# A four-layer diffusion transformer on one core: one operation less in the differential bias, shared accumulation for the last units, earlier splits of gated tiles

## The chip, the core and the metric

The program runs on one NeuronCore of a Trainium2 chip. The metric is the device time of one execution in microseconds (us). The engines are TensorE (PE; its weight loads are PEld), VectorE (DVE), ScalarE (ACT), GpSimd (POOL) and SyncE (SP, which issues the transfers). A lower time is better.

## What is computed

Four layers (`DEPTH = 4`) act on 1024 latent tokens and 256 context tokens, each 1024 wide, batch one. Layer i uses the mixer i mod 3: A (grouped-query attention, layers 0 and 3), B (neighbourhood attention with a learned bias, layer 1), C (differential attention, layer 2).

```
def diff_attention(q, k, v, lam):
    scale = HEAD_DIM ** -0.5
...
        logits = jnp.einsum("bqhmd,bkhmd->bhmqk", qb, k).astype(jnp.float32) * scale
        p = jax.nn.softmax(logits, axis=-1)
        a = (p[:, :, 0] - lam * p[:, :, 1]).astype(v.dtype)
        return jnp.einsum("bhqk,bkhd->bqhd", a, v)
```

Every layer does: modulated norm, one input projection to the mixer's q, k, v and a SiLU gate, the mixer, the gate times the mixer's output, an output projection, a gated residual. Layers 0 to 2 also carry the context tokens; layer 3 only produces the latent ones. In layer C each head has two softmax maps over context and latent keys, and the second, times a learned `lam`, is added to the first (the kernel's `lam` carries the sign). Each softmax subtracts the row's maximum, so the exponential's bias is `-SC` times the largest score over context and latent keys.

## The kernel before

**Numbers and layout.** Matmuls that need more than one pass of accuracy take each operand as a rounded high part and a low remainder: `round_pool` (L130, on POOL) writes the high part, `sub` (L133, on DVE) subtracts it from the original and writes the low part. `whi` and `wlo` are such parts of a weight, the two `ogt` buffers are those of a gated tile. Tokens go in tiles of 128, eight latent and two of context.

**Layers A (0 and 3).** Attention is done in units: a pair of heads for a block of up to 512 query tokens, over 10 key blocks for latent queries, 2 for context ones. Units come in the order in which the groups `g` = 0 to 3 are written. For each key block PE writes the transposed scores `st` (L714, L715), ACT exponentiates them to `p` (L719, 128x1024), PE accumulates `o` (L739). The softmax's denominator is the sum of all `p` of the unit: POOL adds most of them into one accumulator (L753), DVE adds the last ones into a second (the same line, `side` = 1), and `mixed` (L757) multiplies `o` by the gate and adds the two accumulators (L761). Then `spread` multiplies the sum by ones on PE (`sum`, L767), ACT turns it into a reciprocal, `error` and `step` refine it (DVE, ACT), and `over` (L788, L789, POOL) multiplies it into `og`, the gated output. These last five steps of the last unit are the tail: `unit_events` returns it in `self.tail`, and `out_proj` emits it.

Only PE's instructions are pinned in the order in which they are written in layers A; what stands where on the other engines is the scheduler's choice. In layers B and C (`tile_events`) all four compute engines are pinned in the order of the events' times.

**Output projection.** `out_proj` (L875) loops over the work list: the first 512 output columns of every tile, then the second 512. For each entry it needs the gated tile in two parts (`split`: four blocks of 256 columns, so 4 instructions L130 on POOL and 4 L133 on DVE) and does 24 matmuls `y` (L911): 8 slices of the inner dimension by three part products. The split of the next tile is written ahead of the products of the present one. The evacuation is DVE (`yg`, L950), POOL (`xo`, L951), and a transfer.

**Layer C.** A tile is 128 queries of one head. For each, `near` writes the context scores `sc` of both maps, takes their maxima `mx` (L1456, a 128x2 result) and multiplies `mx` by `-SC` (L1457). `scores(m)` writes the latent scores of map m, takes their maximum `ml` (L1466, a 128x1024 reduction) and combines it with `mx` by multiplying with `-SC` and taking the minimum (L1467), one per map. ACT exponentiates with `mx` as bias. `sums` makes the row sums and their ratio `rs` (L1404, L1405), DVE combines half of the latent probabilities (L1492), POOL the context ones and the other half (`combine`: L1412 multiplies by `rs`, L1413 adds). PE turns the result (`pT`) and multiplies by the values.

## Time and profile before

| what | value |
|---|---|
| time, median of 3 runs | 3613.51 us (3613.27 to 3614.67) |
| profiled execution, its own time | 3609.91 us |
| its span | 3608.1 us |
| mean granted clock of PE | 0.985 |
| PE busy | 3471.8 us, 96% |
| PEld, DVE, POOL, ACT busy | 72%, 57%, 53%, 37% |

The span is what the trace covers; 1.8 us of the execution's own time lie around it. The profiled execution is 3.6 us (0.1%) under the median of the runs. All instants below are microseconds from the start of that span. PE is busy for almost the whole span, so that the time of the kernel is PE's work and PE's waits; the stretches where PE waits are short and lie at particular places: the ends of the four attentions (around 838, 1686, 2715 and 3505) among them.

### The profile page before, as it was taken

To read this page: it belongs to the slowest core of one execution; us is meant where nothing else is said; L and a number is where in the kernel's file an instruction comes from. 1 tells how busy PE (TensorE), PEld (TensorE's weight loads), DVE (VectorE), ACT (ScalarE), POOL (GpSimd) and SP (SyncE) were. 2 spreads that over 40 slices of the span, in tenths; PEclk is the share of its full clock that TensorE was granted. 3 is DMA by queue.
4 is the path that set the end of the run, shared out by engine and by line. 5 is a ranking of instruction groups with operands and counts; after the bars stand their busy time and mean duration, and the time that the engine had idled before them with its cause. 6 is when DMAs were issued, how large, how long until landed. Compare 5 with 4: busy or idle time off the path is not lost.

```text
span 3608.1 us, 49956 instructions
## 1 busy us (share of the span) xinstructions
PE 3471.8 (96%) x18594; PEld 2608.3 (72%) x18594; DVE 2057.5 (57%) x3358; ACT 1320.9 (37%) x2756; POOL 1915.1 (53%) x1854
## 2 busy tenths in 40 slices
PE   7999999998999999999999999999999999999989
PEld 4887444446788888887878888888887787554447
DVE  5552555665641412888566610799994654466653
ACT  3221444451321212774222211677771322344430
POOL 5540666677531311667565510566775643377884
PEclk9999999999999999999999999999999999999999
DMA  6343443513344434552425531221312335111113
GB/s 211 78 122 101 140 138 113 192 56 97 122 105 129 111 123 113 169 153 69 146 79 140 136 114 56 84 82 44 96 42 95 120 79 142 47 40 44 45 41 88
DMA packets 229453, 370.33 MB, mean 103 GB/s; under 512 B 34088, under 2 KB 124120, under 8 KB 229212
## 3 DMA queue, kind: packets, MB, share of 16 engines
q1 hardware_dynamic: 228636, 367.01, 34.5%
q8 instruction: 147, 2.41, 0.3%
q14 instruction: 94, 0.77, 0.1%
q10 hardware_dynamic: 576, 0.15, 0.0%
HBM read 270.36 MB, written 96.57 MB: 102 GB/s over the span
## 4 chain that ended last, share of the span: by engine, by line
PE 73%; DVE 14%; POOL 7%; issue 3%; ACT 1%; DMA 1%; SPq 0%; POOLq 0%; ACTq 0%; DVEq 0%
PE proj L382 22%; PE zT L467 11%; PE y L911 9%; PE o L739 7%; PE st L714 4%; PE st L715 4%; DVE ml L1466 3%; PE sl L670 2%; PE o L1136 2%; POOL p L753 2%; DVE wlo L133 1%; PE qkT L437 1%; POOL rstd L146 1%; PE ada L195 1%; PE pT L1214 1%
## 5 line engine op out<-in xcount | busy, mean ns | idle before, releaser
L753 POOL TENSOR_TENSOR p<-p,p 128x1024 f32<-128x1024 f32 x224 | 540.1, 2411 | 303.6 <-PE o L739 258.2
L382 PE MATMUL proj<-whi,hhi 128*128 128x512 f32 x1408 | 556.3, 395 | 3.7 <-POOL whi L130 2.4
L382 PE MATMUL proj<-wlo,hhi 128*128 128x512 f32 x1408 | 550.8, 391 | 3.0 <-DVE wlo L133 3.0
L382 PE MATMUL proj<-whi,hlo 128*128 128x512 f32 x1408 | 550.4, 391 | 0.0
L719 ACT ACTIVATE p<-st 128x1024 f32<-128x1024 f32 (+1 forms) x336 | 324.1, 1003 | 286.2 <-PE st L715 274.3
L911 PE MATMUL y<-whi,ogt 128*128 128x512 f32 x1216 | 387.5, 396 | 13.2 <-POOL ogt L130 9.4
L661 DVE TENSOR_REDUCE M<-sl 128x1 f32<-128x512 f32 (+1 forms) x326 | 209.8, 685 | 293.2 <-PE sl L670 243.5
L133 DVE TENSOR_TENSOR wlo<-wraw,whi 128x1024 fp32r<-128x1024 f32 x136 | 217.3, 1612 | 221.6 <-POOL whi L130 196.3
L739 PE MATMUL o<-p,v 128*64 128x512 f32 x1344 | 321.2, 599 | 0.0
L130 POOL TENSOR_SCALAR whi<-wraw 128x1024 fp32r<-128x1024 f32 x136 | 178.7, 1319 | 252.6 <-DMA wraw<-in_c_w_in_dram 86.0
L382 PEld LDWEIGHTS proj<-whi,hhi 128*128 128x128 f32 x1408 | 265.7, 189 | 57.9 <-POOL whi L130 2.6
L382 PEld LDWEIGHTS proj<-wlo,hhi 128*128 128x128 f32 x1408 | 265.6, 189 | 57.6 <-DVE wlo L133 4.7
L382 PEld LDWEIGHTS proj<-whi,hlo 128*128 128x128 f32 x1408 | 265.3, 188 | 55.2
L911 PEld LDWEIGHTS y<-whi,ogt 128*128 128x128 f32 x1216 | 229.8, 189 | 67.8 <-POOL ogt L130 11.6
L467 PE MATMUL zT<-hhi,whi 128*128 128x512 f32 (+1 forms) x704 | 256.9, 365 | 5.6 <-DVE qklo L133 5.6
L404 ACT ACTIVATE y<-proj 128x1024 f32<-128x1024 f32 (+1 forms) x68 | 65.6, 964 | 527.0 <-PE proj L382 469.4
L467 PE MATMUL zT<-hhi,wlo 128*128 128x512 f32 (+1 forms) x704 | 254.5, 362 | 1.3 <-DVE wlo L133 1.3
L467 PE MATMUL zT<-hlo,whi 128*128 128x512 f32 (+1 forms) x704 | 254.5, 362 | 0.0
L911 PE MATMUL y<-wlo,ogt 128*128 128x512 f32 x608 | 238.6, 392 | 0.0
L146 POOL TENSOR_TENSOR rstd<-rstd,mhalf 128x16 f32<-128x16 f32 (+3 forms) x132 | 231.0, 1750 | 10.9
L714 PE MATMUL st<-q,k 128*128 128x512 f32 x512 | 217.8, 425 | 10.5 <-DVE M L658 7.2
L658 DVE TENSOR_REDUCE M<-sl 128x2 f32<-128x1024 f32 (+1 forms) x165 | 200.6, 1216 | 45.2 <-PE sl L670 40.1
(221 smaller groups left out, 7035.2 us busy)
## 6 DMA issues: line engine op xcount, KB each, us to landing
adaw<-in_ada_w_dram SPq DMA_DIRECT2D x96, 512.0 KB
xo<-xres SPq DMA_DIRECT2D x86, 256.0 KB
wraw<-in_a_w_in_dram SPq DMA_DIRECT2D x40, 512.0 KB
k<-k SPq DMA_DIRECT2D x40, 512.0 KB
q<-qkhi SPq DMA_DIRECT2D x76, 256.0 KB
q<-qklo SPq DMA_DIRECT2D x76, 256.0 KB
q<-q SPq DMA_DIRECT2D x136, 128.0 KB
wraw<-in_b_w_in_dram SPq DMA_DIRECT2D x32, 512.0 KB
```

The costliest lines, as they stand in the source:

```text
L130: self.nc.gpsimd.tensor_scalar(out=out, in0=in_, scalar1=1.0, scalar2=0.0, op0=ALU.mult, op1=ALU.add)
L133: self.nc.vector.tensor_tensor(out, a, b, op=ALU.subtract)
L146: nc.gpsimd.tensor_tensor(r, r, self.mhalf[:, :n], op=ALU.pow)
L382: nc.tensor.matmul(ps[:, i, :], self.h_op(a, 2 * tp + i, k), wop(b, k), start=(k == 0 and j == 0), stop=(k == KT - 1 and j == 2),)
L467: nc.tensor.matmul(ps, wop(a, k)[:, b * P : (b + 1) * P], self.h_cols(c, g, k), start=(k == 0 and j == 0), stop=(k == KT - 1 and j == 2),)
L658: nc.vector.tensor_reduce(out=out, in_=both.rearrange("p (h q k) -> p h q k", h=2, q=n), axis=AX.X, op=ALU.max)
L661: nc.vector.tensor_reduce(out=out[:, hh, :], in_=ps[hh].rearrange("p (q k) -> p q k", q=n), axis=AX.X, op=ALU.max)
L714: nc.tensor.matmul(ps[:, hh, :], self.k_op(K, 0, kt), q1[:, hh, :], start=True, stop=False)
L719: nc.scalar.activation(p, ps, AF.Exp, scale=HD**-0.5)
L739: nc.tensor.matmul(st["o"][hh * HD : (hh + 1) * HD, :], v(hh, kt), p[:, hh, :], start=j == 0, stop=j == N - 1, tile_position=(0, hh * HD),)
L753: eng.tensor_tensor(a, a, p, op=ALU.add)
L911: nc.tensor.matmul(ps, ot[a][:, k, :], wop[h](b, k), start=(k == 0 and j == 0), stop=(k == KT - 1 and j == 2))
```

## The change

There are five edits.

1. In layer C the multiplication of `mx` by `-SC` (L1457) is dropped. The combination in `scores` becomes one `tensor_scalar`: the larger of `ml` and the column `mx[:, m]`, times `-SC`. Before, it was a `scalar_tensor_tensor` with two tensor operands and a constant; now it has one tensor operand, a per-partition scalar that is read from memory, and a constant.
2. In layers A the number of key blocks that DVE adds is an argument, `share`: 5 for the units of the last group with `t0 > 0` (two units in each of the layers 0 and 3), 2 for all others as before. Of the 10 blocks of such a unit POOL adds 4 instead of 7 times, DVE 4 times instead of once.
3. Splitting a tile is a method, `split_tile`. In layers 0, 1 and 3 (`kind < 2`) the first two gated tiles are split by events at 0.965 to 0.99 of the attention's length.
4. In `out_proj`, layer 2's first two tiles are split inside the loop behind the first step of the weights' second half.
5. The tail of the last unit is emitted behind the second `y` tile (`i > 0`) instead of behind the first.

```diff
-            side = int(j > 0 and j >= N - 2)
+            side = int(j > 0 and j >= N - share)
...
+    def split_tile(self, t):
+
+        if t in self.halves:
+            return
+        self.halves[t] = hi, lo = [self.slot([P, KT, P], F32R, "ogt") for _ in range(2)]
+        g, o = t // 4, (t % 4) * P
+        for b in range(4):
+            a = self.og.block(b, g)[:, :, o : o + P]
+            h, l = (x[:, 2 * b : 2 * b + 2, :] for x in (hi, lo))
+            self.round_pool(h, a)
+            self.sub(l, a, h)
+
...
-        start(0)
         for i, (h, t) in enumerate(work):
             cs = slice(h * 512, h * 512 + 512)
             if i < len(steps):
                 steps[i]()
-            if i + 1 < len(work):
-                start(i + 1)
+            for x in work[i : i + 2]:
+                self.split_tile(x[1])
...
-            products(ps, h, halves[t] if h == 0 else halves.pop(t), range(KT))
-            while self.tail:
+            products(ps, h, self.halves[t], range(KT))
+            while self.tail and i > 0:
                 self.tail.pop(0)()
...
-                        2 * g + pr, t0, n, kts, self.finish_plain,
+                        2 * g + pr, t0, n, kts, 5 if g == 3 and t0 else 2, self.finish_plain,
...
-                nc.vector.tensor_scalar_mul(mx, mx, -SC)
...
-                nc.vector.scalar_tensor_tensor(
-                    out=mx[:, m : m + 1], in0=ml, scalar=-SC, in1=mx[:, m : m + 1], op0=ALU.mult, op1=ALU.min
+                nc.vector.tensor_scalar(
+                    out=mx[:, m : m + 1], in0=ml, scalar1=mx[:, m : m + 1], scalar2=-SC, op0=ALU.max, op1=ALU.mult
                 )
...
+            if kind < 2:
+                extra.append((0.965, 0.99, [lambda t=t: self.split_tile(t) for t in range(2)]))
             self.og = self.Mixed(self)
+            self.halves = {}
```

The order of the instructions moves at three places that matter below.

On POOL at the end of layer 0's attention before the change (the `p` are accumulations, `r` and `og` the end of the unit before, `whi` weights, `ogt` the splits of the first two gated tiles):

```order
L753 TENSOR_TENSOR p_6213<-p_6213,p_6220 128x1024
L753 TENSOR_TENSOR p_6213<-p_6213,p_6234 128x1024
L753 TENSOR_TENSOR p_6213<-p_6213,p_6241 128x1024
L753 TENSOR_TENSOR p_6213<-p_6213,p_6263 128x1024
L753 TENSOR_TENSOR p_6213<-p_6213,p_6272 128x1024
L788 TENSOR_TENSOR r_6252<-r_6252,e_6265 128x512
L789 TENSOR_TENSOR og_626<-og_626,r_6252 128x512
L753 TENSOR_TENSOR p_6213<-p_6213,p_6296 128x1024
L753 TENSOR_TENSOR p_6213<-p_6213,p_6303 128x1024
L130 TENSOR_SCALAR whi_6371<-wraw_6185 128x1024
L130 TENSOR_SCALAR ogt_6439<-og_617 128x256
```

The same place on POOL with the change:

```order
L753 TENSOR_TENSOR p_6212<-p_6212,p_6219 128x1024
L753 TENSOR_TENSOR p_6212<-p_6212,p_6234 128x1024
L753 TENSOR_TENSOR p_6212<-p_6212,p_6241 128x1024
L753 TENSOR_TENSOR p_6212<-p_6212,p_6263 128x1024
L788 TENSOR_TENSOR r_6252<-r_6252,e_6265 128x512
L789 TENSOR_TENSOR og_626<-og_626,r_6252 128x512
L130 TENSOR_SCALAR ogt_6349<-og_617 128x256
```

Three accumulations are gone from POOL's queue, and the split of the first gated tile stands directly behind `og`. On DVE the last unit's accumulations stand with the change like this, among the low parts of the two tiles:

```order
L753 TENSOR_TENSOR p_6272<-p_6272,p_6296 128x1024
L753 TENSOR_TENSOR p_6272<-p_6272,p_6303 128x1024
L133 TENSOR_TENSOR ogt_6350<-og_617,ogt_6349 128x256
L133 TENSOR_TENSOR ogt_6350<-og_620,ogt_6349 128x256
L133 TENSOR_TENSOR ogt_6350<-og_622,ogt_6349 128x256
L133 TENSOR_TENSOR ogt_6350<-og_625,ogt_6349 128x256
L753 TENSOR_TENSOR p_6272<-p_6272,p_6329 128x1024
L133 TENSOR_TENSOR ogt_6385<-og_617,ogt_6384 128x256
L753 TENSOR_TENSOR p_6272<-p_6272,p_6336 128x1024
L133 TENSOR_TENSOR ogt_6385<-og_620,ogt_6384 128x256
L759 TENSOR_TENSOR og_626<-o_6243,og_626 128x512
L761 TENSOR_TENSOR p_6212<-p_6212,p_6272 128x1024
```

All four accumulations are DVE's now, and the tail's sum (L761) comes behind one and a half split tiles.

On DVE at the end of layer 1's attention before the change (`ptl` copies turned probabilities out of PE's banks, `mx` is the last latent tile's maximum, the two ISA operations add the bias and take maxima, `mc` is the maximum for the context queries):

```order
L1215 COPY ptl_14572<-pT_14573 128x768
L1162 TENSOR_REDUCE mx_14592<-sc_14587 128x2
L1173 ISA p_14599,ml_14600<-st_14594,biasb_14032 128x256
...
L1197 RECIPROCAL rs_14620<-rs_14620 128x2
L1215 COPY ptl_14633<-pT_14634 128x768
L1243 TENSOR_REDUCE mc_14657<-sc_14648 128x4
```

The same place on DVE with the change (lines stand 10 earlier in the file):

```order
L1205 COPY ptl_14572<-pT_14573 128x768
L133 TENSOR_TENSOR ogt_14588<-og_9876,ogt_14587 128x256
L133 TENSOR_TENSOR ogt_14588<-og_10035,ogt_14587 128x256
L133 TENSOR_TENSOR ogt_14588<-og_10217,ogt_14587 128x256
L133 TENSOR_TENSOR ogt_14588<-og_10270,ogt_14587 128x256
L1152 TENSOR_REDUCE mx_14602<-sc_14597 128x2
...
L1187 RECIPROCAL rs_14630<-rs_14630 128x2
L1205 COPY ptl_14643<-pT_14644 128x768
L133 TENSOR_TENSOR ogt_14653<-og_9876,ogt_14652 128x256
L133 TENSOR_TENSOR ogt_14653<-og_10035,ogt_14652 128x256
L133 TENSOR_TENSOR ogt_14653<-og_10217,ogt_14652 128x256
L133 TENSOR_TENSOR ogt_14653<-og_10270,ogt_14652 128x256
```

The split of tile 0 now stands between the copy `ptl` and the maximum `mx`, that of tile 1 ahead of the maximum `mc`; before, tile 0's stood behind all of the attention's operations but one. On POOL the high parts stand behind the two multiplications of `p` by `rs` that belong to the tile of the first copy and of the second.

## Rows read from the trace of the kernel before

**Rows 1.** The page's first part: busy time by engine, share of the span, instructions

```profile
PE 3471.8 (96%) x18594; PEld 2608.3 (72%) x18594; DVE 2057.5 (57%) x3358; ACT 1320.9 (37%) x2756; POOL 1915.1 (53%) x1854
```

**Rows 2.** Waits of PE, 780 to 870: total us, times, longest

```profile
PE sum L767 <- DVE p L761: 11.2, 2, 9.1
```

**Rows 3.** Timeline of POOL, end of layer 0's attention: start, duration, what, count

```profile
807.86 14.02 POOL L753 TENSOR_TENSOR p<-p,p 128x1024 f32<-128x1024 f32 x5
...
824.42 4.79 POOL L753 TENSOR_TENSOR p<-p,p 128x1024 f32<-128x1024 f32 x2
```

**Rows 4.** Timeline of DVE, the same stretch, idle time before in brackets

```profile
802.21 2.43 DVE L753 TENSOR_TENSOR p<-p,p 128x1024 f32<-128x1024 f32 x1 [5.68 <-ACT p L719]
...
834.37 1.41 DVE L753 TENSOR_TENSOR p<-p,p 128x1024 f32<-128x1024 f32 x1
```

**Rows 5.** Timeline of PE: the sums of the last two units of layer 0

```profile
809.01 1.08 PE L767 MATMUL sum<-p,ones 128*64 128x512 f32 x4 [2.11 <-DVE p L761]
...
837.66 1.97 PE L767 MATMUL sum<-p,ones 128*64 128x512 f32 x4 [9.05 <-DVE p L761]
```

**Rows 6.** Waits of PE, 3440 to 3545, end of layer 3's attention

```profile
PE y L911 <- POOL ogt L130: 9.1, 3, 7.8
...
PE sum L767 <- DVE p L761: 1.3, 1, 1.3
```

**Rows 7.** Timeline of POOL, the same stretch

```profile
3484.28 14.00 POOL L753 TENSOR_TENSOR p<-p,p 128x1024 f32<-128x1024 f32 x5
```

**Rows 8.** Timeline of PE: the first `y` of layer 3

```profile
3507.87 0.80 PE L911 MATMUL y<-whi,ogt 128*128 128x512 f32 x1 [7.83 <-POOL ogt L130]
```

**Rows 9.** Timeline of DVE, end of layer 1's attention

```profile
1672.03 0.94 DVE L1215 COPY ptl<-pT 128x768 f32<-128x768 f32 x1
1672.88 0.68 DVE L1162 TENSOR_REDUCE mx<-sc 128x2 f32<-128x512 f32 x1
...
1684.01 2.86 DVE L133 TENSOR_TENSOR ogt<-og,ogt 128x256 fp32r<-128x256 f32 x4
```

**Rows 10.** Timeline of POOL, the same stretch

```profile
1673.18 1.15 POOL L1142 TENSOR_SCALAR p<-p,rs 128x384 f32<-128x384 f32 x2
...
1683.57 1.85 POOL L130 TENSOR_SCALAR ogt<-og 128x256 fp32r<-128x256 f32 x4
```

**Rows 11.** Timeline of PE: last products of layer 1's attention, ahead of the first `y`

```profile
1685.79 1.08 PE L1136 MATMUL o<-pt,vl 128*64 128x256 f32 x8 [1.11 <-ACT pt L1271]
```

**Rows 12.** Waits of PE, 2705 to 2740, end of layer 2's attention

```profile
PE pT L1562 <- POOL p L1413: 2.6, 2, 1.4
...
PE o L1418 <- ACT pc L1516: 1.7, 1, 1.7
```

**Rows 13.** Groups by form, 2269 to 2705, layer 2's attention: busy, mean ns | idle before

```profile
L1457 DVE TENSOR_SCALAR mx<-mx 128x2 f32<-128x2 f32 x64 | 31.0, 484 | 2.2
L1467 DVE SCALAR_TENSOR_TENSOR mx<-ml,mx 128x1 f32<-128x1 f32 x128 | 27.4, 214 | 4.4
...
L1372 POOL MEMSET k<- 1x1024 f32 x14 | 12.8, 944 | 0.4
```

**Rows 14.** The chain that ended last, the same stretch, shares by line

```profile
by line: DVE ml L1466 24.2%; issue 7.8%; DVE pt L1509 7.5%; DVE mx L1456 6.4%; DVE mx L1457 5.9%; PE o L1418 4.4%; DVE mx L1467 4.1%; DVE p L1492 3.6%; DVE rs L1405 2.8%; PE st L1398 2.5%; PE st L1399 2.5%; POOL p L1413 2.3%; DVE og L1438 2
```

**Rows 15.** Instructions of single lines: ns minimum/median/maximum

```profile
L1457 DVE TENSOR_SCALAR mx<-mx x64: 168/431/1229, 2269.0 to 2698.4; 128x2 f32<-128x2 f32 x64
L1467 DVE SCALAR_TENSOR_TENSOR mx<-ml,mx x128: 158/159/860, 2270.5 to 2701.4; 128x1 f32<-128x1 f32 x128
L1405 DVE SCALAR_TENSOR_TENSOR rs<-rs,lam,cs x72: 219/219/457, 2278.0 to 2710.0; 128x1 f32<-128x1 f32 x64, 128x2 f32<-128x2 f32 x8
```

**Rows 16.** Timelines of DVE and of POOL in one ordinary tile of layer 2

```profile
2430.30 0.43 DVE L1457 TENSOR_SCALAR mx<-mx 128x2 f32<-128x2 f32 x1
...
2431.89 0.21 DVE L1467 SCALAR_TENSOR_TENSOR mx<-ml,mx 128x1 f32<-128x1 f32 x1
...
2430.79 1.28 POOL L1413 TENSOR_TENSOR p<-p,p 128x512 f32<-128x512 f32 x1
```

More of the change, by code (lines that the diff above doesn't have):

```diff
@@ L625, with softmax_unit @@
         pass
-    def softmax_unit(self, qscr, heads, Ks, vsrc, og, pair, t0, n, kts, finish):
+    def softmax_unit(self, qscr, heads, Ks, vsrc, og, pair, t0, n, kts, share, finish):
         nc = self.nc
@@ L725, in softmax_unit, with finish_plain @@
         u.scores = [lambda j=j, kt=kt: scores(j, kt) for j, kt in enumerate(kts)]
-        u.products, u.ends = finish(st, kts, n, pair, t0, og)
+        u.products, u.ends = finish(st, kts, n, pair, t0, og, share)
         return u
-    def finish_plain(self, st, kts, n, pair, t0, og):
+    def finish_plain(self, st, kts, n, pair, t0, og, share):
         nc = self.nc
@@ L897, in load @@
             return full, x
-        def split(t, blocks, ot):
-            g, o = t // 4, (t % 4) * P
-            for b in blocks:
-                a = og.block(b, g)[:, :, o : o + P]
-                hi, lo = (x[:, 2 * b : 2 * b + 2, :] for x in ot)
-                self.round_pool(hi, a)
-                self.sub(lo, a, hi)
         def products(ps, h, ot, ks):
@@ L913, in products @@
                     )
-        def parts():
-            return [self.slot([P, KT, P], F32R, "ogt") for _ in range(2)]
         work = [(h, t) for h in range(2) for t in tiles]
         ready = [load(*work[0]), load(*work[1])]
-        halves = {}
-        def start(i):
-            t = work[i][1]
-            if t not in halves:
-                halves[t] = parts()
-                split(t, range(4), halves[t])
-        start(0)
         for i, (h, t) in enumerate(work):
```

## The prediction

> **What bounds the kernel now.** I read the page first, for which engine fills the span; then PE's waits by stretch, for where it is held up; there the timelines of the engines it waits for; and for layer 2 the groups and the chain, because there no single wait stands out. PE is busy for 96% of the span [rows 1], so an edit pays only where it shortens a wait of PE, or, in layer 2's attention, the round that DVE, POOL and PE go through for every tile.
>
> At the end of layer 0's attention PE waits 11.2 us for the accumulated `p`, 9.1 of it before the last unit's sum [rows 2]. POOL is the late engine: its first five additions of that unit run 14.02 us without a break and two more follow up to 829.2 [rows 3], while DVE, which makes one, ends it only at 835.8 [rows 4]. In layer 3 the same queue holds up something else: POOL's additions [rows 7] come before the first gated tile's split, and the first `y` waits 7.8 us, all such waits together 9.1, the sum 1.3 [rows 6, 8]. At layer 1's end PE is nearly full: 1.11 us of waiting ahead of the last products, and `y` follows [rows 11]. At layer 2's end PE waits 2.6 us for POOL and 1.7 us for ACT [rows 12]. In layer 2's attention the last chain is mostly DVE, with 5.9% on the dropped line [rows 14].
>
> **The change, part by part.** The terms are against the profiled execution's own 3609.9 us.
>
> *Layer 0's end (share, tail).* Per unit three POOL additions go; at 14.02/5 = 2.8 us that is 8.4 us of queue. DVE gets three more, at 1.41 us alone and 2.43 beside POOL [rows 4]: 4 to 7 us on an engine that was waiting. POOL no longer finishes the chain, and the tail's sum moves behind 24 more `y` matmuls (about 6 us of PE work). I take both sum waits as gone but for 0.5 us: -10.7. After the 9.05 us wait four sums took 1.97 us instead of 1.08 [rows 5], the pace of the lower clock level; this 0.9 goes with the wait, and as much again (estimate) for the matmuls behind it. Together **-12.5** (-8 to -14). Cover: the splits of tiles 0 and 1 must be ready before the additions that now stand between them on DVE; if the third tile's split is late, 1.5 us come back, the upper end.
>
> *Layer 3's end.* The waits are 9.1 + 1.3 = 10.4 us [rows 6], with about 1.8 for the slower matmuls behind the long one as in layer 0 (estimate; the first `y` took 0.80 us [rows 8]): 12.2. What is late next: DVE's queue. A weight's low part now stands behind eight split parts and an addition, and `yg` of the first tile behind four late additions and `mixed`, so that POOL's `xo`, and with it the third tile's split queued behind it, wait. I leave 3.2 us for these: **-9** (-5 to -12).
>
> *Layer 1's end (early split).* Nothing is added, but queues here are fixed. DVE's four `ogt` of tile 0 now stand ahead of the last tile's `mx`, which ran at 1672.88 [rows 9]; their POOL halves stand behind the `p` that POOL ends at 1673.18 + 1.15 = 1674.33 [rows 10]. POOL's start to DVE's end took 1686.87 - 1683.57 = 3.3 us for such a group [rows 9, 10]. So `mx` starts near 1677.6, 4.7 us late. Behind it in DVE's queue are the next `rs`, POOL's next `p`, and then tile 1's split, again behind that `p` and ahead of `mc`: by the same sum another 4.7 us. PE has nothing but this attention's turns and products to do here, so it waits too; before, the split lay beside the last turns and cost nothing. Upper bound 9.4 plus 1.6 for a lower clock, 11; lower bound 3, if only one group falls on the path. The later `y` waits of some 0.8 us go. I take **+8**.
>
> *Layer 2's end.* The first tile's split no longer alternates with POOL's and DVE's last attention operations. Of 2.6 + 1.7 = 4.3 us of waits [rows 12] I take **-2.5** (-4 to 0).
>
> *Layer 2's attention.* 64 operations of L1457 go, 31.0 us of DVE time at 484 ns [rows 13]. Alone one takes 168 ns [rows 15], so 20 of the 31 us are waiting: in [rows 16] it ends when POOL has finished what it was at. In the same tile the next small operation, L1467, starts at 1.89 and ends at 2.10, with POOL's addition at 0.79 + 1.28 = 2.07 (counted from 2430). So the two small operations wait for the same addition, and dropping the first lets the second arrive 0.4 us earlier at a gate that opens no sooner. Of the 64 first ones I count 37 that overlap such an addition; the remaining 27, at the dropped line's median of 0.43 us, gain at most 11.6. PE has to have the scores ready for that; half is 5.8. Against it the new operation reads its scalar from memory. The nearest row is L1405, 219 ns with such a scalar against L1467's 158 with a constant [rows 15]: 61 ns on 64 second operations and some 27 first ones, 5.6. Bounds: nothing is held and all of L1457's chain time goes, 5.9% of 436 us = -26 [rows 14]; or no gain and the scalar on all 128, +8. The row that it is nearest to is the single tile, which gives nothing: 5.6 - 5.8, with the odd tile that has more to give, **-1** (-12 to +8).
>
> A rule of the Trainium skill (SBUF — State Buffer, section "Who interferes with whom") says that a DVE operation with two SBUF inputs contends with GpSimd only while that reads SBUF, but a `tensor_scalar` in a mode that uses both ports contends with GpSimd whatever it does, and is blocked until that instruction ends. The first half of it would be the old L1467, the second the new operation. The trace agrees on the dropped L1457, which ends with POOL's work [rows 16]; what the rule would do here beyond the sum is a rival below.
>
> *Sum:* -12.5 - 9 + 8 - 2.5 - 1 = -17.0. The profiled execution stands 3.6 us under the median, so 3592.9 there and 3613.5 - 17.0 = **3596.5** as a median. A difference of 0.2%, 7.2 us, is about what a measurement of this kernel tells from none.
>
> **The rivals.**
> - *The new operation takes no turn with POOL* (one tensor input instead of two). Then the gate of [rows 16] is gone: C gives -12 when PE's scores limit it, -26 when the chain's full share goes: 3585.5 to 3571.5. For it: only the operation with two tensors and the 128x2 form are known to wait. Against: L1457 has one input and waits. Chance 0.20.
> - *Layer 1 hides the split.* If its two DVE stalls fall into waits that the trace does not show, +8 becomes 0: 3588.5. Against: the queue is fixed, and DVE is late already. Chance 0.10.
> - *The additions only change their queue.* DVE and POOL exclude each other on two-input additions (2.43 against 1.41 us, [rows 4]); if DVE's four come as late as POOL's seven did, half to all of the 21.5 us of layers 0 and 3 stays: 3607 to 3618. Against: DVE idled before its one addition [rows 4] while POOL ran seven. Chance 0.12.
> - *Slower: the new operation is held in both uses like L1457, which was itself free.* If what L1457 waited for now falls on L1467's place in every tile, 128 operations cost 0.484 instead of 0.214 us, +34.6 with no credit, or +17.3 if only the second ones change: 3613.5 - 16.0 + 17.3 = 3614.8, up to 3632. It decides from a mean of 0.214 + 16/128 = 0.34 us for the new operation, and past 0.40 the kernel is slower by 0.2%. For it: L1457 is held in most of its 64 cases (mean 484, alone 168 ns). Against: L1467's second operations meet an idle POOL (the median in [rows 15] is the minimum). Chance 0.10.
> - *The new operation also waits for POOL's memsets.* They write one row and read nothing; 14 of 0.94 us lie in the stretch [rows 13], at most 13 us, and half of that, 6.5, if every other one meets a small operation: 3603 to 3609.5. That is what the page named above would have; no row here has such an operation beside a memset. Chance 0.06.
>
> **How the numbers follow.** The forecast has 0.42. Its terms' bounds, taken as independent (root of the sum of their squares), reach 12.6 below and 11.5 above it: 3584 to 3608 is its own range. The rivals have 0.20, 0.10, 0.12, 0.10 and 0.06. Faster by over 0.2% (under 3606.3): 0.40 of the 0.42, then 0.20, 0.10, a third of 0.12 and most of 0.06, together 0.78. Slower by over 0.2% (over 3620.7): half of the fourth rival, 0.05. The rest, 0.17, is within 0.2%. The range of 8 in 10 runs from 3574, which leaves out the far end of the first rival (0.03), to 3613, which leaves out the fourth and the far half of the third (0.16).
>
> **What would show it.** In layer 0: no wait of PE ahead of the `sum` above 1 us, and the first `y` some 10 us earlier after the scores. In layer 3: the first `y` no later than 2 us behind the last `o`. In layer 1: DVE idle for some 3 to 4 us twice, each ended by POOL's `ogt`, and waits of PE near 1674 to 1686 that were 1 us and are 8 together. In layer 2's attention: the stretch as long as before within 10 us, the new operation ending with POOL's addition in most tiles. I am wrong if that stretch shortens by over 12 us, if the new operation ends while an addition of POOL runs, or if layer 1's end takes no longer than before.

## The result, and the profile after

The changed kernel takes 3582.61 us (median of 4 runs, 3581.54 to 3583.28) against 3613.98 us of the kernel before on the same chips (4 runs): ratio 0.9915, 95% interval 0.9902 to 0.9927, 31.4 us less. That is inside the range, and 14 us better than the forecast of 3596.5. The profiled execution's span is 3581.0 us, 27.1 less than before; it took 3582.7 us itself, 0.1 us from the median of its runs, while that of before (3609.9) lies 4 us under its median, so the traces show 4 us less than the medians.

The page's first part of the changed kernel, to set beside [rows 1]:

```profile
PE 3463.8 (97%) x18594; PEld 2599.3 (73%) x18594; DVE 2042.9 (57%) x3306; ACT 1321.7 (37%) x2756; POOL 1878.7 (52%) x1842
```

Since PE's order is nearly the same in both programs, the place of the gain can be read by setting the start of the same matmul in one trace against that in the other. The difference changes at a few places and stays nearly constant between them:

| stretch | forecast | measured, us |
|---|---|---|
| start to the end of layer 0's attention | 0 | +3.2 |
| layer 0's end and first `y` tiles (780 to 910) | -12.5 | -5.6 |
| layer 1's end | +8 | +7.4 |
| layer 2's attention, first score to the last tile's turn | -1 | -25.1 |
| layer 2's end, up to the first `y` | -2.5 | -3.0 |
| layer 3's end | -9 | -4.5 |
| all else | 0 | +0.5 |
| sum | -17.0 | -27.1 |

Layer 1 and layer 2's end came out as worked out, the ends of the layers 0 and 3 at half, and layer 2's attention gave nearly all that the chain's share had promised (5.9% of 436 us in [rows 14]): the first rival, with a chance of 0.20.

Single traces carry these rows only so far. In the four runs below that change layer 2 alone, layer 3's end, whose code is the old one, still differs from the kernel before by +0.1 to +1.8 us; in three of the last four, which have the same code in layer 0, its end stands at -5.0, -5.2 and -6.6. So a row of the table holds to some 2 us, and that of layer 2's attention to 4 (see below).

**Layer 2's attention.** The small operations by group in the changed kernel, 2274 to 2690 (compare [rows 13]; L1456 is the new operation, L1395 the ratio `rs`, L1479 the row sums), then the new operation's shortest, median and longest (compare [rows 15]), then one tile on DVE and on POOL (compare [rows 16]):

```profile
L1456 DVE TENSOR_SCALAR mx<-ml,mx 128x1 f32<-128x1 f32 x128 | 27.4, 214 | 4.5
...
L1395 DVE SCALAR_TENSOR_TENSOR rs<-rs,lam,cs 128x1 f32<-128x1 f32 x64 | 17.1, 267 | 2.4 <-DVE rs L1394 0.2
L1479 DVE TENSOR_TENSOR cs<-sm 128x2 f32<-128x2 f32 x64 | 12.7, 199 | 0.0
```

```profile
L1456 DVE TENSOR_SCALAR mx<-ml,mx x128: 212/214/217, 2275.5 to 2681.3; 128x1 f32<-128x1 f32 x128
```

```profile
2426.96 1.21 DVE L1455 TENSOR_REDUCE ml<-st 128x1 f32<-128x1024 f32 x1
2428.21 0.22 DVE L1456 TENSOR_SCALAR mx<-ml,mx 128x1 f32<-128x1 f32 x1
...
2427.57 1.29 POOL L1403 TENSOR_TENSOR p<-p,p 128x512 f32<-128x512 f32 x1
```

The new operation ends at 2428.43, while POOL's addition runs on to 2428.86. Its longest case is 217 ns: it is never held, in all 128 cases. 38 of them lie wholly within such an addition of POOL, 7 within one of the memsets. Before, the dropped line was held for 20 us and the kept one for 7.2 (busy time less the minimum for each case).

**Layer 1's end.** DVE's timeline of the changed kernel, with the wait ahead of each split (compare [rows 9]), and PE's wait for the first maximum that comes late:

```profile
1669.56 0.94 DVE L1205 COPY ptl<-pT 128x768 f32<-128x768 f32 x1
1672.27 2.85 DVE L133 TENSOR_TENSOR ogt<-og,ogt 128x256 fp32r<-128x256 f32 x4 [1.77 <-POOL ogt L130]
1675.05 0.68 DVE L1152 TENSOR_REDUCE mx<-sc 128x2 f32<-128x512 f32 x1
...
1677.18 0.94 DVE L1205 COPY ptl<-pT 128x768 f32<-128x768 f32 x1
1679.90 2.02 DVE L133 TENSOR_TENSOR ogt<-og,ogt 128x256 fp32r<-128x256 f32 x4 [1.78 <-POOL ogt L130]
1681.84 1.21 DVE L1233 TENSOR_REDUCE mc<-sc 128x4 f32<-128x1024 f32 x1
```

```profile
PE sc L1230 <- DVE ml L1163: 3.8, 1, 3.8
```

From the end of the copy at 1670.50 to `mx` at 1675.05 DVE does the split and the waiting for it: 4.6 us (4.7 in the prediction). The second group takes 3.7 us from 1678.12 to 1681.84. All of PE's waits from 1655 to 1720 were 2.5 us before and are 7.5 now.

**Layer 0's end.** DVE's timeline of the changed kernel (compare [rows 4]) and PE's waits (compare [rows 5]):

```profile
820.32 4.16 DVE L753 TENSOR_TENSOR p<-p,p 128x1024 f32<-128x1024 f32 x2 [0.52 <-PE o L739]
824.77 2.86 DVE L133 TENSOR_TENSOR ogt<-og,ogt 128x256 fp32r<-128x256 f32 x4 [0.30 <-POOL ogt L130]
827.56 1.41 DVE L753 TENSOR_TENSOR p<-p,p 128x1024 f32<-128x1024 f32 x1
...
831.89 1.21 DVE L761 TENSOR_TENSOR p<-p,p 128x1024 f32<-128x1024 f32 x1
```

```profile
833.25 1.98 PE L767 MATMUL sum<-p,ones 128*64 128x512 f32 x4 [3.81 <-DVE p L761]
...
857.07 0.50 PE L914 MATMUL y<-whi,ogt 128*128 128x512 f32 x1 [1.06 <-POOL ogt L130]
```

The sum waits 3.8 us where I left 0.5, and its four matmuls still take 1.98 us: the granted clock is 0.50, the lower level (1.2 GHz), from 833 to 837, after PE had been busy for 0.4 of the 4 us ahead of it. DVE is the late engine now, and what makes it late are the split parts among its additions.

**Layer 3's end.** PE's waits between 3418 and 3520 in the changed kernel (compare [rows 6]):

```profile
PE y L914 <- POOL ogt L130: 3.2, 3, 2.0
PE y L914 <- DVE ogt L133: 1.7, 2, 0.9
PE y L914 <- DVE wlo L133: 1.4, 1, 1.4
```

The first `y` follows the last `o` without a wait (7.8 us before [rows 8]). What comes back is 1.4 us for a weight's low part and 3.2 and 1.7 for the splits of the tiles after it, 6.3 us in all, where I left 3.2.

### The profile page after: what moved, and what is told of

It is laid out like the page before. It is cut to its first block, busy times and chain, and to the rows that moved or that the text cites. A ratio compares the mean times of both kernels' runs of the same rounds, so it can differ in the third digit from the quotient of the medians.

```text
span 3581.0 us, 49893 instructions
## 1 busy us (share of the span) xinstructions
PE 3463.8 (97%) x18594; PEld 2599.3 (73%) x18594; DVE 2042.9 (57%) x3306; ACT 1321.7 (37%) x2756; POOL 1878.7 (52%) x1842
## 4 chain that ended last, share of the span: by engine, by line
PE 79%; DVE 9%; POOL 6%; issue 3%; ACT 1%; DMA 1%; SPq 0%; ACTq 0%; POOLq 0%; DVEq 0%
PE proj L382 21%; PE zT L467 12%; PE y L914 9%; PE o L739 8%; PE st L714 5%; PE st L715 4%; PE o L1408 3%; PE sl L670 2%; PE o L1126 2%; DVE wlo L133 1%; POOL rstd L146 1%; PE qkT L437 1%; PE st L1388 1%; PE st L1389 1%; PE pT L1493 1%
## 5 line engine op out<-in xcount | busy, mean ns | idle before, releaser
L753 POOL TENSOR_TENSOR p<-p,p 128x1024 f32<-128x1024 f32 x212 | 506.6, 2390 | 317.2 <-PE o L739 263.8
L146 POOL TENSOR_TENSOR rstd<-rstd,mhalf 128x16 f32<-128x16 f32 (+3 forms) x132 | 230.8, 1749 | 10.8
```

The lines of the kernel that those rows point to most:

```text
L146: nc.gpsimd.tensor_tensor(r, r, self.mhalf[:, :n], op=ALU.pow)
L753: eng.tensor_tensor(a, a, p, op=ALU.add)
```

## The experiments

After the result the question was what the new operation gained by. **Theory H (holds):** the gain is that nothing in the pair waits for POOL. **Theory Q (queue):** it is one DVE operation less. Four kernels take the kernel before and change the pair; all compute the same output.

**The new operation alone.**

```diff
-                nc.vector.tensor_scalar_mul(mx, mx, -SC)
...
-                nc.vector.scalar_tensor_tensor(
-                    out=mx[:, m : m + 1], in0=ml, scalar=-SC, in1=mx[:, m : m + 1], op0=ALU.mult, op1=ALU.min
+                nc.vector.tensor_scalar(
+                    out=mx[:, m : m + 1], in0=ml, scalar1=mx[:, m : m + 1], scalar2=-SC, op0=ALU.max, op1=ALU.mult
```

> The kernel before with the differential bias in one operation and nothing else changed. In the changed kernel the attention of layer 2 became some 25 us shorter, and the new operation took 212 to 217 ns in all 128 cases, whatever POOL did. Theory H (holds): the gain is that nothing in the pair of small operations waits for POOL any more. Theory Q (queue): the gain is one operation less per tile on DVE, 31 us of busy time. Both expect the attention 24 to 26 us shorter here and the whole kernel at 0.9925 to 0.994 of before; less than 20 us would mean that the shorter attention needs the other edits.

Measured: 3590.89 us, ratio 0.9929 (0.9909 to 0.9948), 22.6 us less; the attention 22.4 us shorter. The ratio is where both expected it; the attention gains 1.6 us less than the 24 to 26 that both named.

**The dropped line alone.**

```diff
-        qtab = self.rope_tables(ins["c_q_g"][j : j + 1])
+        qtab = self.rope_tables(ins["c_q_g"][j : j + 1], -(HD**-0.5))
...
-                nc.vector.tensor_scalar_mul(mx, mx, -SC)
...
-                    out=mx[:, m : m + 1], in0=ml, scalar=-SC, in1=mx[:, m : m + 1], op0=ALU.mult, op1=ALU.min
+                    out=mx[:, m : m + 1], in0=ml, scalar=1.0, in1=mx[:, m : m + 1], op0=ALU.mult, op1=ALU.min
```

The lines above do not show what goes with the turned sign: maxima become minima, the exponentials take -1 as their scale, and POOL multiplies the queries' gain by the factor once. DVE has no operation more by it.

> The dropped line alone: the factor is put into the queries' table ahead of the layer, so that scores come out as minus the scaled ones, and the old two-tensor operation stays as the minimum of the two. It computes the same output. Theory H: what held the dropped line up now holds the kept operation: its mean rises from 0.214 to 0.25 to 0.35 us, and the attention becomes 4 to 12 us shorter, ratio 0.9965 to 0.999. Theory Q: one operation less is one operation less, 22 to 26 us shorter, ratio 0.993 to 0.994.

Measured: 3597.29 us, ratio 0.9953 (0.9939 to 0.9968), the attention 15.6 us shorter. Between the two expectations, so neither holds as it stood. The kept operation's group in this run, 2240 to 2710, and its shortest, median and longest:

```profile
L1473 DVE SCALAR_TENSOR_TENSOR mx<-ml,mx 128x1 f32<-128x1 f32 x128 | 42.4, 331 | 4.4
```

```profile
L1473 DVE SCALAR_TENSOR_TENSOR mx<-ml,mx x128: 158/160/1091, 2275.4 to 2690.6; 128x1 f32<-128x1 f32 x128
```

The holds did pass to it, as theory H says: 42.4 - 128 x 0.158 = 22.2 us, of 27.5 us for the pair before. But the operation's own time, 64 x 0.168 = 10.8 us, was gained, and 5.3 us of the holds: the pair's busy time fell from 31.0 + 27.4 = 58.4 to 42.4, by 16.0 us, and the attention by 15.6.

**The combination alone.**

```diff
-                nc.vector.scalar_tensor_tensor(
-                    out=mx[:, m : m + 1], in0=ml, scalar=-SC, in1=mx[:, m : m + 1], op0=ALU.mult, op1=ALU.min
+                nc.vector.tensor_scalar(
+                    out=mx[:, m : m + 1], in0=ml, scalar1=-SC, scalar2=mx[:, m : m + 1], op0=ALU.mult, op1=ALU.min
```

> The first line is kept, and only the combination becomes a tensor_scalar with a per-partition scalar (times -SC, minimum with the column of mx), with the same result. Theory H: the new form is never held, 0.21 us in all cases; the 7 us of holds on the old one go, 7 us of scalar reads come, and the line ahead is held as before (mean 0.45 to 0.5 us): attention -3 to +3 us, ratio 0.999 to 1.001. Theory Q: same count of operations and a dearer form, +3 to +7 us.

Measured: 3613.85 us, ratio 0.9998 (0.9989 to 1.0007), the attention as long as before (-0.1). Groups of this run, 2240 to 2710:

```profile
L1457 DVE TENSOR_SCALAR mx<-mx 128x2 f32<-128x2 f32 x64 | 32.8, 512 | 2.2
L1467 DVE TENSOR_SCALAR mx<-ml,mx 128x1 f32<-128x1 f32 x128 | 27.4, 214 | 4.5
```

Again never held (212 to 216 ns), at the same 27.4 us in all: what the holds cost before, the scalar from memory costs now. As theory H expected.

**Two columns.**

```diff
-                nc.vector.tensor_scalar_mul(mx, mx, -SC)
+                for m in range(2):
+                    nc.vector.tensor_scalar_mul(mx[:, m : m + 1], mx[:, m : m + 1], -SC)
```

> The multiplication by -SC is done by two operations of one column each with a constant, in place of one of two columns; nothing else changes. If one column is what keeps an operation from being held (theory H, by size), each takes 0.14 to 0.17 us whatever POOL does, 20 us less on the line in all and one more operation: attention 3 to 12 us shorter, ratio 0.9965 to 0.999, the kept operation behind it held more. If it is the scalar read from memory (theory H, by operand), one column with a constant is held like two: means of 0.3 to 0.5 us in the first of each pair, attention +3 to +12 us. Theory Q: +8 to +10 us, one operation more.

Measured: 3602.2 us, ratio 0.9965 (0.9952 to 0.9978), the attention 11.7 us shorter with one operation more per tile. The shortest, median and longest of the divided line (first) and of the kept operation behind it:

```profile
L1458 DVE TENSOR_SCALAR mx<-mx x128: 142/150/156, 2271.8 to 2689.6; 128x1 f32<-128x1 f32 x128
```

```profile
L1468 DVE SCALAR_TENSOR_TENSOR mx<-ml,mx x128: 158/160/1096, 2273.3 to 2692.5; 128x1 f32<-128x1 f32 x128
```

128 operations of one column, none above 156 ns, where 64 of two columns went up to 1229 ns. 104 of the 128 lie wholly within an instruction of POOL. So for a `tensor_scalar` the size decides, not the scalar from memory; a two-tensor operation is held at one column too, as the kept one is here. Theory Q, as a count of operations, is refuted here. The pair's busy time fell from 58.4 to 13.8 + 33.8 = 47.6 us (two columns overlap in the queue), by 10.8, and the attention by 11.7.

The four runs together: the attention follows DVE's whole busy time, holds included. The stretch from the first score to the last latent tile's turn, in the kernel before (first) and the changed one: the window, its length, the busy time of PE, PEld, DVE, ACT and POOL, the granted clock:

```profile
2267.60:2712.20 444.60, 414.61 (x2891) 373.49 (x2890) 415.26 (x839) 328.39 (x937) 305.95 (x421) 0.96 0.22 66
```

```profile
2272.60:2692.20 419.60, 402.01 (x2892) 363.47 (x2890) 392.06 (x775) 329.50 (x938) 304.07 (x420) 0.98 0.23 70
```

| kernel | DVE busy against before, us | length against before, us |
|---|---|---|
| changed kernel | -23.2 | -25.1 |
| new operation alone | -22.7 | -22.4 |
| dropped line alone | -14.6 | -15.6 |
| combination alone | +1.2 | -0.1 |
| two columns | -9.7 | -11.7 |

The pair itself gives 58.4 - 27.4 = 31.0 us; 6 us of its 27.5 us of holds turn up on the next two-tensor operations (`cs` 9.8 to 12.7, `rs` 14.3 to 17.1 us in the changed kernel), and some 2 us more elsewhere on DVE. Seven traces have the same code in this stretch (the changed kernel, the new operation alone, the next four runs and the one with the old order below). Their DVE time agrees to 1.5 us, their length only to 4: -21.3 to -25.3 us against before, -23.0 in the mean. So one for one holds within that scatter, and -25.1 is near its far end. PE, busy for 402 of 419.6 us in the changed kernel, is nearly full there too; whether a still shorter DVE queue would pay is not shown.

The next four take the changed kernel and take back one edit each. For the ends, **theory S** says that the shared additions carry the gain, **theory P** that the early split does.

**Layer 1 without its early split.**

```diff
-            if kind < 2:
+            if kind == 0:
```

> The changed kernel with layer 1's early split taken back (layers 0 and 3 keep it). In the changed kernel's trace DVE stood idle twice behind POOL's high parts at the end of layer 1's attention, and everything after it stood 7.4 us later against the kernel before. If the early split is the cause, the first y of layer 1 stands again at the distance of before from the attention's start, and the kernel takes 7 to 8 us less than the changed one: ratio to before 0.989 to 0.990. If the loss came from a shift that the shorter layer 0 brings along, 0 to 2 us.

Measured: 3576.28 us, ratio 0.9898 (0.9883 to 0.9913). Layer 1's end, up to the `y` that stands at 1712 in the kernel before, now costs +2.6 us against the kernel before instead of +7.4. PE's wait there, ahead of the second matmul of the first `y`:

```profile
PE y L914 <- DVE ogt L133: 2.1, 1, 2.1
```

So the early split is the cause, and some of the loss is left (+2.6 here, +1.0 in the run without any early split, which has the same code at this place); that the rest comes from splitting the first tile behind the weights' first step is shown by the runs with the old order below, where it is 0.0.

**Share 2 everywhere.**

```diff
-                        2 * g + pr, t0, n, kts, 5 if g == 3 and t0 else 2, self.finish_plain,
+                        2 * g + pr, t0, n, kts, 2, self.finish_plain,
```

> The changed kernel with share 2 for all units, so that POOL again makes seven additions of the last units. Theory S (the additions carry the gain of the ends of layers 0 and 3, 5.6 and 4.5 us in the trace): both ends lose most of it, +8 to +12 us against the changed kernel, with waits of 7 to 9 us at the sum of layer 0 and the first y of layer 3. Theory P (the early split carries it): +0 to +3 us.

Measured: 3594.58 us, ratio 0.9946 (0.9931 to 0.996), 12.0 us above the changed kernel by the medians. Layer 0's end is where it was before the change (-0.2 us instead of -5.6), layer 3's 4.4 us longer than before (instead of 4.5 shorter). PE's waits at the two ends:

```profile
PE sum L767 <- DVE p L761: 13.3, 2, 11.2
```

```profile
PE y L914 <- DVE wlo L133: 7.1, 1, 7.1
```

Theory S. In layer 3 the early split without the share even costs, as far as this one trace with the later tail shows it; up to 1.8 of its 4.4 us can be scatter.

**No early split in any layer.**

```diff
-            if kind < 2:
+            if False:
```

> The changed kernel without any early split: the first two tiles are split in the loop of the output projection in all layers. Layer 1 should give back its 7.4 us. Theory S: the ends of layers 0 and 3 move by 0 to 3 us, in sum -4 to -7 us against the changed kernel. Theory P: they lose 8 to 10 us, in sum +1 to +3 us.

Measured: 3575.15 us, ratio 0.989 (0.9874 to 0.9907). Layer 0's end: -6.6 us against the kernel before (-5.6 with the early split), layer 3's -3.3 (-4.5). So the early split is worth nothing in the layers A together, and costs in layer 1. The whole is 4.7 us shorter than the changed kernel in the traces, as theory S expected, and 7.5 by the medians. Layer 0 shows why (PE's timeline): the sum waits half as long and at the full pace, and the split's wait appears at the first `y`.

```profile
828.04 1.08 PE L767 MATMUL sum<-p,ones 128*64 128x512 f32 x4 [1.82 <-DVE p L761]
...
833.62 1.22 PE L914 MATMUL y<-whi,ogt 128*128 128x512 f32 x2 [2.53 <-DVE ogt L133]
```

**The tail behind the first tile.**

```diff
-            while self.tail and i > 0:
+            while self.tail:
```

> The changed kernel with the tail of the last unit behind the first y tile again. In the changed kernel's trace the tail's sum of layer 3 had its operand at 3488.2 and stood at 3489.6; behind the first y tile it would stand near 3484 and wait some 4 us. In layer 0 the operand is there in time (838.2 against 843.8). So +3 to +5 us against the changed kernel, all of it in layer 3; if the later tail matters in layer 0 too, up to +8.

Measured: 3582.45 us, ratio 0.9913 (0.9898 to 0.9928): the changed kernel's own. The wait is there, in layer 3:

```profile
PE sum L767 <- DVE p L761: 4.2, 1, 4.2
```

but the splits behind it then find PE later, and their waits of 4.9 us fall to 0.6 (and the weight's rises from 1.4 to 2.4). The expectation counted the wait and not what it replaces: edit 5 moves a wait and is worth nothing here.

The last four try to put the good parts together.

**Old order of the first split, early split in layer 3 alone.**

```diff
+        self.split_tile(work[0][1])
         for i, (h, t) in enumerate(work):
...
-            if kind < 2:
+            if last:
```

> A version put together from the runs: the changed kernel with the first tile's split ahead of the weights' first step as in the kernel before, and the early split in layer 3 alone. By the trace of the changed kernel and of the run without early splits: 7.4 us back in layer 1 (there the run without early splits got back only 5, with a wait of 2.1 us for the split's low part ahead of the second matmul of the first y, which the old order should remove), 1 us in layer 0. Against the changed kernel -8 to -10 us, ratio to before 0.9875 to 0.9895. If the old order of the split does not matter, the wait of 2.1 us stays and it is -6 to -8.

Measured: 3579.57 us, ratio 0.991 (0.9895 to 0.9925). Against the changed kernel that is 3.0 us less by the medians, where 8 to 10 were expected. Layer 1's end costs nothing now, as expected; but the old order takes back 2.8 us at layer 2's end (19.0 us from the last tile's turn to the first `y`, 16.3 in the changed kernel, 19.2 before), so one order for all layers is right for layer 1 and wrong for layer 2. Layer 0's end is 1.6 us worse than in the run without any early split (-5.0 against -6.6), but it is -6.6 in a run below with the same code there, so this is no effect of the order.

**The factor in the queries' table.**

```diff
-        qtab = self.rope_tables(ins["c_q_g"][j : j + 1])
+        qtab = self.rope_tables(ins["c_q_g"][j : j + 1], -(HD**-0.5))
...
-                    out=mx[:, m : m + 1], in0=ml, scalar1=mx[:, m : m + 1], scalar2=-SC, op0=ALU.max, op1=ALU.mult
+                    out=mx[:, m : m + 1], in0=ml, scalar1=mx[:, m : m + 1], scalar2=None, op0=ALU.min
...
-                nc.vector.tensor_scalar_mul(mx, mx, -SC)
```

This and the last two runs stand on the one with the old order; the lines above again do not show what goes with the turned sign.

> The same, and the factor -SC goes into the queries' table of layer 2, so that the multiplication of the context queries' maxima (128x4, eight times, mean 0.95 us in the changed kernel, nearly all of it held) falls away too; the combination keeps its form with one operation instead of two in it. If layer 2's attention follows DVE's busy time one for one, another -6 to -8 us; if PE is its bound by now, 0 to -3.

Measured: 3580.54 us, ratio 0.9911 (0.9896 to 0.9925): no gain, the attention as long as without it (-22.4 us in both). Eight operations with 7.6 us went, and these grew (this run first, the one without the fold below, 2262 to 2682):

```profile
L1403 DVE SCALAR_TENSOR_TENSOR rs<-rs,lam,cs 128x1 f32<-128x1 f32 x64 | 20.4, 318 | 2.2
L1487 DVE TENSOR_TENSOR cs<-sm 128x2 f32<-128x2 f32 x64 | 15.8, 247 | 0.0
```

```profile
L1396 DVE SCALAR_TENSOR_TENSOR rs<-rs,lam,cs 128x1 f32<-128x1 f32 x64 | 17.9, 279 | 2.2
L1480 DVE TENSOR_TENSOR cs<-sm 128x2 f32<-128x2 f32 x64 | 12.2, 191 | 0.0
```

3.6 + 2.5 = 6.1 us of the 7.6: the hold passed on to the next two-tensor operations, DVE's whole busy time in the stretch fell by 0.6 us, and the length followed it. This is what I had predicted for the main term, and here it is what happened; the first expectation (one for one) took the operation's time and left out that nearly all of it was hold.

**The ratio with one tensor.**

```diff
-            nc.vector.scalar_tensor_tensor(
-                out=r, in0=r, scalar=self.lam, in1=S[:, :, 0], op0=ALU.mult, op1=ALU.mult
+            for i in range(S.shape[1]):
+                nc.vector.tensor_scalar(
+                    out=r[:, i : i + 1], in0=r[:, i : i + 1], scalar1=self.lam, scalar2=S[:, i, 0:1],
```

> The same, and the ratio rs is written as a tensor_scalar with two per-partition scalars in place of the operation with two tensors, whose mean rose from 0.22 to 0.27 us in the changed kernel because POOL holds it in some tiles. If one-column operations with one tensor are never held, its minimum is its maximum, near 0.27 us by the 56 ns that a scalar from memory cost; no change of time within 2 us. If two scalars bring the hold back, single cases above 0.5 us.

Measured: 3578.42 us, ratio 0.9905 (0.989 to 0.992): within the run's scatter of the one before. Mean 272 ns with two scalars, no gain.

**Share 4.**

```diff
-                        2 * g + pr, t0, n, kts, 5 if g == 3 and t0 else 2, self.finish_plain,
+                        2 * g + pr, t0, n, kts, 4 if g == 3 and t0 else 2, self.finish_plain,
```

> The second of these with share 4 in place of 5: POOL makes five additions of the last units, DVE three. In the run without early splits POOL's fourth addition of layer 0's last unit ended at 816.7 and DVE's last at 826.6, so DVE is the later of the two, and the sum waited 1.8 us for it. If DVE's queue sets the sum, one addition less on it takes 1 to 2 us off; if POOL's splits behind its additions set the first y, +1 to +3 us in each of the layers 0 and 3.

Measured: 3578.56 us, ratio 0.9906 (0.989 to 0.9923). PE's wait at layer 0's end:

```profile
PE sum L767 <- DVE p L761: 5.7, 1, 5.7
```

The sum waits 5.7 instead of 1.7 us: for layer 0 neither expectation. DVE's timeline there says why:

```profile
823.02 1.41 DVE L133 TENSOR_TENSOR wlo<-wraw,whi 128x1024 fp32r<-128x1024 f32 x1 [6.53 <-POOL whi L130]
```

A weight's low part stands ahead of DVE's additions, and POOL makes its high part behind the fifth addition: DVE stands idle for 6.5 us with its own additions queued behind. The first `y` tiles then wait less, so that layer 0's end is no worse (-6.1 us, between the -5.2 and -6.6 of the two runs before it); layer 3's is 1.6 us worse, which is no more than its scatter.

None of these beats the run without any early split (3575.15 us). That one is below both kernels: 7.5 us under the changed kernel's median, though the two were timed in different sets of runs and their intervals against the kernel before overlap (0.9874 to 0.9907 and 0.9902 to 0.9927).

## Why the prediction was right and where it was wrong

- **Layer 2's attention (-1 forecast, -25.1 measured): wrong, and the largest error.** Two steps failed. The first is that the new operation would wait at POOL's addition like the dropped one: the row chosen for it was L1457, with two columns, and the operation has one. It was never held, and the run with two columns shows that one column is enough. The rival that came true gave one tensor input as the reason; the runs show that the one column is needed as well. The second is "the two small operations wait for the same addition", and with it "a gate that opens no sooner". In the tile of [rows 16] the dropped line ended at 2430.73, before the addition began at 2430.79; what had just ended was POOL's multiplication ahead of it:

```profile
2430.02 0.69 POOL L1412 TENSOR_SCALAR p<-p,rs 128x512 f32<-128x512 f32 x1
```

Of the 46 dropped lines that were held, 23 end with such a multiplication and 11 with the 128x512 addition, and in none of the 64 tiles did both small operations wait for the same instruction of POOL. In the run with the dropped line alone 22.2 us of holds stayed, and the attention still became 15.6 us shorter. Why the gate then opens sooner was not tested by itself: POOL's multiplications wait for DVE's `rs` of the same round (0.73 us of POOL's idle time at 2425.06 in the changed kernel ends with it), so the likely reason is that the round comes earlier when DVE has less to do. The chain's share of 5.9%, which I had only for the bound, came nearest, but it is no price of the line: with the line alone gone, 15.6 of its 26 us were gained.

- **The scalar from memory** was priced rightly: 61 ns forecast from L1405, 214 - 158 = 56 ns measured, in all 128 cases and not in 91 (64 + 27).
- **The memset rule** (the Trainium skill, SBUF — State Buffer, "Who interferes with whom"): by it a `tensor_scalar` in a mode with both ports would have been blocked by the memsets, at most 13 us. Seven new operations ran within a memset, none above 217 ns, so the rule's condition was not met by an operation of one column; for the two-column one, held up to 1229 ns beside POOL's other work, the trace agrees with it, though none of the two-column ones met a memset.
- **Layer 0's end (-12.5 forecast, -5.6 measured): right mechanism, wrong size.** POOL's queue was the cause and DVE took the additions over; the term that was mis-sized is "both sum waits as gone but for 0.5 us": 3.8 us stayed, with the lower clock behind it, because the split parts stand among DVE's additions. Without them it is 1.8 us and full clock. The 1.5 us for late splits came too (1.1 and 0.9).
- **Layer 3's end (-9 forecast, -4.5 measured): right mechanism, wrong size.** The first `y` came as forecast; the waits that come back are 6.3 and not 3.2 us; the 1.4 us beyond that are no more than the scatter of this stretch.
- **Layer 1's end (+8 forecast, +7.4 measured): right**, with both stalls where they were worked out (each 1.8 us of idle time and the split itself, where 3 to 4 us of idle time had been named), and taken back by taking the split back, the last part of it by the old order.
- **Layer 2's end (-2.5 forecast, -3.0 measured): right**; the old order of the split undoes 2.8 us of it.
- **Edit 5** I had costed inside layer 0; the run without it shows no difference above 0.7 us in either layer, which is within the scatter.

The forecast of 3596.5 was 14 us high: 24 us were missed in layer 2's attention and 11 us too many were expected of the layers 0 and 3; the rest are the steps of the table that no edit explains and the 4 us between trace and median. Two of the three signs of being wrong came: the stretch shortened by over 12 us, and the new operation ended while an addition ran. That the sum is off by 14 us and not by 24 is luck: the gain missed in layer 2 was set against gains that did not come in the layers 0 and 3. The range held because the first rival had been given the chain's share as its far end.

## What to carry to other kernels

Take the row that prices a new operation from one of the same size and operand count, and if there is none at that size, measure: here a row with two columns, taken for an operation of one, was the first step of the largest error. In a loop over engines, one tile shows where an operation waits but not what a shorter queue is worth; the engine's whole busy time in the stretch does, counted after the change, with the holds where they have gone: a hold that is taken away must be looked for on the next operation that can be held. In a queue of fixed order, work that is moved ahead of a latency chain costs its own wait for the other engine, even if the engine that is short of work (PE here) seems far away.

## What was not expected of the hardware

- A `tensor_scalar` on one value per partition was never held by POOL: 128 with constants at 142 to 156 ns and 128 each at 212 to 217 ns in three of the kernels shown, whatever POOL did. The same operation on 128x2 was held up to 1229 ns, and a two-tensor operation of one column up to 1096 ns.
- Executions differ where the code does not. Between 360 and 365 the kernel before and the changed one run the same instructions; the stretch's rows of the kernel before (first) and of the changed one, with the granted clock behind the busy times:

```profile
360.00:365.00 5.00, 4.38 (x20) 2.10 (x20) 3.29 (x6) 2.05 (x2) 0.16 (x1) 1.00 0.07 24
```

```profile
360.00:365.00 5.00, 4.55 (x14) 2.66 (x12) 2.42 (x3) 2.04 (x3) 0.00 (x0) 0.59 0.15 59
```

The clock is at 1.00 in one and 0.59, a mean over both levels, in the other, and 2.3 us are lost there. Other runs with the same code up to this point show either value (+3.4 us for the new operation alone by 400, +0.9 for the combination alone). Such steps of 1.5 to 2.4 us, here, near 2900 and near 3100, are why terms of 2 us can't be told from single traces, and they make up most of the 3.2 us in the first row of the table.
